# One decoder layer on one core: other row groups in the opening, part of its sums added by VectorE, and all its turns made by spaced transfers

## The chip, the cores and the metric

The kernel runs on one core of one Trainium2 chip. The metric is the device time in microseconds (us) of one launch. TensorE (PE) multiplies into PSUM; VectorE (DVE) and ScalarE (ACT) do elementwise work; GpSimd (POOL) does a few multiplies and issues some transfers; SyncE (SP) issues nearly all DMA transfers from one queue, in the order of the program.

## The reference

One layer for 256 tokens of width 2048 in float32. Every sub-layer is modulated by columns that are computed from a vector c through the large matrix w_ada (2048 x 9*2048).

```
mod = (silu(c) @ w_ada + b_ada).reshape(9, 2048)
h = rms_norm(x) * (1 + mod[1]) + mod[0]
x = x + 0.5 * mod[2] * swiglu(h, w_ffn1_gu, w_ffn1_down)     # d_ff = 5632
h = rms_norm(x) * (1 + mod[4]) + mod[3]
x = x + mod[5] * token_mixing(h, w_in, ...)                  # retention beside window attention
h = rms_norm(x) * (1 + mod[7]) + mod[6]
x = x + 0.5 * mod[8] * swiglu(h, w_ffn2_gu, w_ffn2_down)
out = rms_norm(x)

def swiglu(h, w_gu, w_down):
    gate, up = split(h @ w_gu, 2)
    return (silu(gate) * up) @ w_down
```

## The kernel before

Every large product is made in three parts. A weight tile (128 rows x 512 columns, two row blocks at a time) is split into a high half, cast by ScalarE (`wh`, L375), and a low half, subtracted by VectorE (`wl`, L377). The activations are held in the same two halves (`hh`, `hl`), and TensorE adds high by high, low by high and high by low into a bank of PSUM (`products`, L360). A row block is 128 of the 2048 rows of h; it takes six products of 512 columns per chunk of 512 output columns (three parts, two token tiles).

The columns of `mod` are made by VectorE: a row of w_ada (transposed, 1024 KB) is loaded and multiplied with silu(c) and summed (`ada_pass`, L220), in one, two or four passes of 2048, 1024 or 512 elements.

The first SwiGLU cannot start with the whole of h, since each row block of h needs its own two rows of `mod` (m = 1 and 0). So its first 16 chunks (eight pairs of gate and up, `EARLY = 8`) are opened in groups of row blocks. `bounds` says which blocks a group holds. In each group, every chunk is visited once (`visit`): the group's blocks are loaded (`load_blocks`, up to four blocks in a raw buffer), split and multiplied into the chunk's two banks. After a group but the last, the sums are copied out of PSUM by ScalarE (`to_parts`, L1219), and in the next group they are copied back into the banks ahead of the products (`open_banks`, L1191; the name for it there is seeded). The last group adds the saved parts when it applies SwiGLU (`swiglu_up`). The first group leaves its last two chunks (1 and 0) in their banks, and the third its last two as well.

While a group is visited, the generator `group` prepares the row blocks of the next one: it loads the rows of w_ada into the two halves of one slot (`ring`), makes the passes, and modulates the normed and transposed x. The transposed x comes from TensorE for the blocks below `TURNED` (`turned_x`) and from a load of transposed x with a multiply on GpSimd for the others (`normed_columns`).

The rows of the other columns (`ROWS_FFN1`: 3 x 16 rows of four passes, 192 passes) are spread over the work by `set_pace` and `tick`: each tick adds a rate, and each whole step is one pass. Before, the third group makes 48 of them, using one half of `ring`, and the last group 16 more, from raw buffers; the remaining 128 are spread over 117 halves of the chunks of `ffn_up` and the down product that follow.

`swiglu_up` has two ways to turn its result for the down product. With `by_dma`, ScalarE takes the two 16-bit planes of a tile apart (L535), SP issues a DMA transpose (L540), and ScalarE puts the planes together (L551); `later` spreads these steps over the following visits by `turn_step`. Otherwise TensorE transposes it (L518). Before, the first six of the eight pairs use DMA and the last two TensorE.

The order of SP is that of the program. The other engines' order outside a few parts written by hand is laid out by a planner from its own estimate of times; `tc.issue_after` only puts an instruction behind another. Pools: four raw buffers of 1 MB, three weight buffers, four banks of PSUM for sums, four slots, five `t512` tiles, three `flat` and four `back` tiles.

Of the kernel before, what the change touches and what calls it, by code (L numbers as in the profile page):

```python
# [9 lines left out]
F32 = mybir.dt.float32  # L10
# [3 lines left out]
ALU = mybir.AluOpType  # L14
# [3 lines left out]
P = 128  # L18
# [59 lines left out]
def layer_kernel(  # L78
# [55 lines left out]
    def t512():  # L134
        return tmp.tile([P, CH], F32, tag="t512", name=nm("t"))
# [497 lines left out]
    def parts_of_h(held, k, h):  # L633

        h = h.rearrange("p (k s) -> p k s", s=S)
        nc.scalar.copy(held.hi[:, k : k + 2, :], h)
        nc.vector.tensor_sub(held.lo[:, k : k + 2, :], h, held.hi[:, k : k + 2, :].bitcast(F32))

    def add_gated(bank, t, c0, gate, ssq):

# [10 lines left out]
    def later(work, then=None, quick=False):  # L651

        (a0, t0, m0), (a1, t1, m1) = work
        order = [a0, a1, None, None, None, t0, t1, None, m0]
        for f in order[:7] + order[7 + quick :]:
            yield
            if f is not None:
                f()
        m1()
        if then is not None:  # L660
            then()

    def later_by_pairs(work):

# [30 lines left out]
    def swiglu_up(banks_g, banks_u, tiles, ci, parts=None, by_dma=False, behind=None):  # L695

        k0 = ci * KB
        dest = tiles[k0 // KD].rearrange("p (k s) -> p k s", s=S)
        kk = k0 % KD
        work = []  # L700
        for t in range(NT):
            s = t512()
            g, u = banks_g[t], banks_u[t]
            if parts is not None:
                nc.vector.tensor_add(s, g, parts[0][t])
                nc.vector.tensor_add(parts[1][t], u, parts[1][t])
                g, u = s, parts[1][t]
            with nullcontext() if behind is None else tc.issue_after(behind):
                nc.scalar.activation(s, g, AF.Silu)
            nc.vector.tensor_mul(s, s, u)  # L710
            if by_dma:
                work.append(turn_by_dma(dest[:, kk : kk + KB, t * P : (t + 1) * P], s))
                continue
            transpose_to(
                dest[:, kk : kk + KB, t * P : (t + 1) * P],
                lambda j: s[:, j * P : (j + 1) * P],
                KB,
            )
        if work:
            turns.append(later(work))  # L720

    def ffn_up(held, w, tiles, first, bg=None, turned=(), ahead=None):
        for ci in range(first, DFF // CH):
# [252 lines left out]
        return [part[(n - 2) // 4][:, at + t * CH : at + (t + 1) * CH] for t in range(NT)]  # L976

    early = [ada_sums() for _ in range(2)]
    rows_of, alone = {}, [False]

    def place(m, k):
        if k < 1:
            rows_of[m, k] = raw_row()
        else:
            if not alone[0]:
                ring.reverse()
            rows_of[m, k] = ring[0]
        ada_load(m, k, rows_of[m, k], 2 if k < 2 else 1)

# [33 lines left out]
            op0=ALU.mult, op1=ALU.add, accum_out=dest,  # L1023
        )

    def turned_x(k0):

        xn = [t512()[:, : 2 * P] for _ in range(NT)]
        for t in range(NT):
            nc.scalar.mul(xn[t], x_sb[:, t, k0 * P : (k0 + 2) * P], r[:, t : t + 1])  # L1030
        turned = [bank()[:, :S] for _ in range(2)]
        for i in range(2):
            for t in range(NT):
                nc.tensor.transpose(
                    turned[i][:, t * P : (t + 1) * P], xn[t][:, i * P : (i + 1) * P], ident
                )
        return turned

    TURNED = 6
    root_row = []  # L1040

    def roots_in_rows():
# [9 lines left out]
            nc.tensor.matmul(rows_ps[:, :S], full, diag[:, :S], start=True, stop=True)  # L1052
        nc.scalar.copy(root_row[0], rows_ps[:, :S])

    def normed_columns(k0):

        xt = t512()
        both = xt.rearrange("p (k s) -> p k s", s=S)
        nc.sync.dma_start(both, x_t[k0 : k0 + 2].rearrange("k p s -> p k s"))
        nc.gpsimd.tensor_tensor(  # L1060
            out=both, in0=both, in1=root_row[0][:, None, :].broadcast_to([P, 2, S]), op=ALU.mult
        )
        return [xt[:, i * S : (i + 1) * S] for i in range(2)]

    def group(ks, passes=2):

        for k0 in ks[::2]:
            srcs = normed_columns(k0) if k0 >= TURNED else None
            for k in (k0, k0 + 1):
                for m in (1, 0):  # L1070
                    if (m, k) not in rows_of:
                        place(m, k)
                    for q in range(passes):
                        ada_pass(k, rows_of[m, k], early[m], q, passes)
                    yield
            for m in (1, 0):
                ada_end(m, slice(k0, k0 + 2), early[m], 0 if m else None, passes)
            h = t512()
            for i, src in enumerate(srcs or turned_x(k0)):
                modulated(h[:, i * S : (i + 1) * S], k0 + i, src, 0)  # L1080
            parts_of_h(held, k0, h)

    banks, moved, unlinted, fresh = {}, set(), set(), set()
    for n, one_bank in zip(firsts, (acc_bank, side_bank)):
        banks[n] = [one_bank() for _ in range(NT)]

# [17 lines left out]
    with tc.manual_schedule(engines=ORDERED):  # L1104
# [41 lines left out]
        modulated(h[:, S:], 1, first_x[1], 0)  # L1146
        parts_of_h(held, 0, h)
        whole_products(1, h)
    bounds = (0, 2, 6, 12, 16)
    groups = [range(a, b) for a, b in zip(bounds, bounds[1:])]  # L1150


# [27 lines left out]

    def open_banks(n, sums):
        seeded = sums and n in moved
        banks[n] = [acc_bank() for _ in range(NT)]
        unlinted.discard(n)
        fresh.add(n)
        if seeded:
            unlinted.add(n)
            fresh.discard(n)
            for b, p in zip(banks[n], part_of(n)):
                with tc.issue_after(cast[-1]):  # L1190
                    nc.scalar.copy(b, p)  # L1191
# [23 lines left out]

    def to_parts(n):
        for p, b in zip(part_of(n), banks.pop(n)):
            with tc.issue_after(cast[-1]):
                nc.scalar.copy(p, b)  # L1219
        moved.add(n)  # L1220

    ROWS_FFN1 = [(2, None, 0.5), (4, 1, None), (3, None, None)]
# [2 lines left out]
    def place_row():  # L1225
        return row_ring[0]() if row_ring else raw_row()

    def place_early():
        if row_ring:
            return row_ring[0]()  # L1230
        return ring[1] if alone[0] else raw_row()

    for g, ks in enumerate(groups):
        alone.append(g == len(groups) - 2)
        del alone[:-1]
        final = g == len(groups) - 1
        if g == len(groups) - 2:
            set_pace(ROWS_FFN1, 192, place_early, 0)
        if final:
            pace["rate"], pace["ahead"] = 1.0, 1  # L1240
        order = chunks if (len(groups) - g) % 2 else chunks[::-1]
        coming = iter(()) if final else group(groups[g + 1], 1 if g == 0 else 2)
        due = 0 if final else 2 * len(groups[g + 1])
        stay = () if final else order[-2:]
        for i, n in enumerate(order):
            if g == 0 and n in firsts:
                continue
            visit(n, ks, n not in stay, g == len(groups) - 2 or final and i < 8, final or (g == len(groups) - 2 and n in stay))
            if g:
                after = [(m, ks) for m in order[i + 1 : i + 2]]  # L1250
                if not after and not final:
                    after = [(n, groups[g + 1])]
                for m, ms in after:
                    ready(m, ms)
                    if m not in banks and not final:
                        open_banks(m, not (g == len(groups) - 2 and m in stay))
            if final:
                turn_step()
            last = len(order) - 2
            if g == 0:  # L1260
                by = [min(due, -(-j * due // 12)) for j in (i - 2, i - 1)]
                by = by[1] - by[0]
            else:
                by = (i + 1) * due // last - i * due // last if i < last else i == last
            for _ in range(by + (g == 0 and i == last)):
                next(coming, None)
            if g == 0:
                for m in {2: firsts[:1], 3: (order[2], firsts[1])}.get(i, order[i - 1 : i]):
                    if m not in stay:
                        to_parts(m)  # L1270
                if i == 3:
                    columns_rest()
                if i == 5:
                    roots_in_rows()
            if n in stay or g == 0:
                continue
            if not final:
                to_parts(n)
            elif n % 2:
                swiglu_up(  # L1280
                    banks.pop(n - 1),
                    banks.pop(n),
                    tiles,
                    n // 2,
                    (part_of(n - 1), part_of(n)),
                    n // 2 < 6,
                    cast[-1],
                )
    gate = gate_row()
    tiles.append(slot())  # L1290
    row_ring.append(two_rows())
    pace["rate"] = (192 - 64) / 117
    pace["ahead"] = AQ
    ffn_up(held, gu, tiles, EARLY, turned=range(EARLY, DFF // CH))
    gate_in = gate_load(gate, 2)
# [473 lines left out]
```

## Time and profile before

| | us |
|---|---|
| median of three timed executions | 2367.28 (2357.96, 2367.28, 2367.73) |
| the profiled execution | 2357.64 |
| its span, first to last instruction | 2355.5 |
| TensorE busy | 2335.7 (99%) |
| VectorE busy | 1673.1 (71%) |
| ScalarE busy | 1367.2 (58%) |
| read from HBM | 598.47 MB, 256 GB/s over the span |

Busy times are shares of the span, and the duration of a pipelined product overlaps the next one's. A window's row gives for each engine the busy us and, in brackets, the number of instructions, then TensorE's granted clock (1.00 is full speed), the mean busy share of the 16 DMA engines and the GB/s they moved. A group of instructions is told by line, engine, operation and tile, then busy us and mean ns of one, then the idle time just before them and what ended it. A wait's row has total us, times and the longest.

### The profile page before, as it was taken

To read this page: it belongs to the slowest core of one execution; us is meant where nothing else is said; L and a number is where in the kernel's file an instruction comes from. 1 tells how busy PE (TensorE), PEld (TensorE's weight loads), DVE (VectorE), ACT (ScalarE), POOL (GpSimd) and SP (SyncE) were. 2 spreads that over 40 slices of the span, in tenths; PEclk is the share of its full clock that TensorE was granted. 3 is DMA by queue.
4 is the path that set the end of the run, shared out by engine and by line. 5 is a ranking of instruction groups with operands and counts; after the bars stand their busy time and mean duration, and the time that the engine had idled before them with its cause. 6 is when DMAs were issued, how large, how long until landed. Compare 5 with 4: busy or idle time off the path is not lost.

```text
span 2355.5 us, 28357 instructions
## 1 busy us (share of the span) xinstructions
PE 2335.7 (99%) x10445; PEld 1918.6 (81%) x10445; DVE 1673.1 (71%) x2576; ACT 1367.2 (58%) x1888; POOL 18.3 (1%) x27
## 2 busy tenths in 40 slices
PE   8999999999999999999999999999999999999998
PEld 5888888888888888778888888888888888888887
DVE  7788888778867768976777776676555555555656
ACT  6766567455556567774556564465455454455544
POOL 0000000000000000000000000000000000000000
PEclk9999999999999999999999999999999999999999
DMA  9989889988765889876778787754767768666553
GB/s 383 375 323 361 355 294 328 336 306 293 302 237 220 293 267 255 258 212 254 267 273 306 288 310 281 272 204 179 259 237 256 242 239 268 223 231 202 193 197 125
DMA packets 191901, 630.24 MB, mean 268 GB/s; under 512 B 113105, under 2 KB 114769, under 8 KB 121233
## 3 DMA queue, kind: packets, MB, share of 16 engines
q1 hardware_dynamic: 189266, 617.41, 74.6%
q0 software_dynamic: 1600, 9.83, 1.0%
q8 instruction: 82, 1.34, 0.2%
q10 hardware_dynamic: 896, 1.19, 0.1%
q14 instruction: 57, 0.47, 0.1%
HBM read 598.47 MB, written 4.22 MB: 256 GB/s over the span
## 4 chain that ended last, share of the span: by engine, by line
PE 96%; DMA 2%; DVE 1%; ACT 1%; issue 0%; SPq 0%; DVEq 0%; ACTq 0%
PE pa L360 93%; DMA raw<-in_w_ffn_gu_dram 1%; DMA rows_x<-in_w_ada_dram 1%; PE ps L1453 0%; DVE slot L220 0%; PE pd L1369 0%; DVE wl L377 0%; ACT wh L375 0%; DMA x_sb<-in_x_dram 0%; PE ps L360 0%; PE pa L1099 0%; PE ps L895 0%; PE pd L1099 0%; DVE rows_x L220 0%; PE ps L1369 0%
## 5 line engine op out<-in xcount | busy, mean ns | idle before, releaser
L377 DVE TENSOR_TENSOR wl<-raw,wh 128x1024 fp32r<-128x1024 f32 x792 | 963.5, 1225 | 511.0 <-ACT wh L375 451.6
L375 ACT CAST wh<-raw 128x1024 fp32r<-128x1024 f32 x792 | 830.6, 1054 | 818.7 <-PE pa L360 752.6
L360 PE MATMUL pa<-wh,hh 128*128 128x512 f32 x2184 | 597.0, 391 | 3.0 <-ACT wh L375 1.7
L360 PE MATMUL pa<-wh,hl 128*128 128x512 f32 x2184 | 592.6, 389 | 0.0
L360 PE MATMUL pa<-wl,hh 128*128 128x512 f32 x2184 | 586.2, 390 | 0.2
L360 PEld LDWEIGHTS pa<-wh,hh 128*128 128x128 f32 x2184 | 407.5, 188 | 91.6 <-ACT wh L375 2.9
L360 PEld LDWEIGHTS pa<-wl,hh 128*128 128x128 f32 x2184 | 409.4, 188 | 86.7 <-DVE wl L377 1.0
L360 PEld LDWEIGHTS pa<-wh,hl 128*128 128x128 f32 x2184 | 409.8, 188 | 86.1 <-issue 0.4
L360 PE MATMUL pa<-wh,a 128*128 128x512 f32 x1824 | 452.1, 389 | 0.0
L360 PEld LDWEIGHTS pa<-wh,a 128*128 128x128 f32 x1824 | 341.7, 188 | 70.6
L360 PE MATMUL pa<-wl,a 128*128 128x512 f32 x912 | 245.1, 389 | 0.0
L220 DVE CUSTOM_DVE_ANT_0 slot<-slot,cact 128x512 f32<-128x512 f32 (+2 forms) x288 | 219.3, 812 | 30.0 <-DMA slot<-in_w_ada_dram 29.5
L360 PEld LDWEIGHTS pa<-wl,a 128*128 128x128 f32 x912 | 171.1, 188 | 35.4
L551 ACT COPY slot<-back 128x512 uint16<-128x512 uint16 x148 | 98.7, 766 | 0.0
L220 DVE CUSTOM_DVE_ANT_0 rows_x<-rows_x,cact 128x512 f32<-128x512 f32 x124 | 78.7, 686 | 18.0 <-DMA rows_x<-in_w_ada_dram 17.8
L410 ACT CAST a<-slot 128x512 fp32r<-128x512 f32 x114 | 70.6, 620 | 29.3 <-PE pa L360 29.0
L535 ACT COPY flat<-t 128x512 uint16<-128x512 uint16 x136 | 76.7, 617 | 8.9 <-DVE t L1526 5.7
L411 DVE TENSOR_TENSOR a<-slot,a 128x512 fp32r<-128x512 f32 x114 | 77.8, 684 | 0.3 <-ACT a L410 0.3
L220 DVE CUSTOM_DVE_ANT_0 raw<-raw,cact 128x512 f32<-128x512 f32 (+1 forms) x92 | 60.7, 709 | 14.6 <-DMA raw<-in_w_ada_dram 14.5
L1219 ACT COPY slot<-pa 128x512 f32<-128x512 f32 x72 | 38.6, 589 | 21.2 <-PE pa L360 21.0
L360 PE MATMUL pa<-wh,home 128*128 128x512 f32 x160 | 39.5, 389 | 0.0
L220 DVE DVE_READ_ACCUMULATOR2_ANT sums<- 128x1 f32 x440 | 35.9, 82 | 0.0
(232 smaller groups left out, 1087.0 us busy)
## 6 DMA issues: line engine op xcount, KB each, us to landing
raw<-in_w_ffn_gu_dram SPq DMA_DIRECT2D x160, 1024.0 KB, 5.5
raw<-in_w_in_dram SPq DMA_DIRECT2D x104, 1024.0 KB, 5.8
raw<-in_w_ffn_down_dram SPq DMA_DIRECT2D x88, 1024.0 KB, 4.9
slot<-in_w_ada_dram SPq DMA_DIRECT2D x87, 1024.0 KB, 7.4
rows_x<-in_w_ada_dram SPq DMA_DIRECT2D x31, 1024.0 KB, 7.1
raw<-in_w_ada_dram SPq DMA_DIRECT2D x22, 1024.0 KB, 5.7
raw<-in_w_swa_branch_dram SPq DMA_DIRECT2D x16, 1024.0 KB, 5.0
raw<-in_w_ret_branch_dram SPq DMA_DIRECT2D x16, 1024.0 KB, 5.4
```

Source lines behind the costliest of these rows:

```text
L220: nc.vector.tensor_tensor_reduce(out=w[:, at], in0=w[:, at], in1=cact[:, at], scale=1.0, scalar=0.0, op0=ALU.mult, op1=ALU.add, accum_out= ...
L360: product = nc.tensor.matmul(banks[t], act[:, j, t * P : (t + 1) * P], weights[:, j, :], start=starts and i == 0 and j == 0, stop=ends and ...
L375: cast.append(nc.scalar.copy(hi, src).ins)
L377: low.append(nc.vector.tensor_sub(lo, src, hi.bitcast(F32)).ins)
L410: nc.scalar.copy(hi, v)
L411: nc.vector.tensor_sub(lo, v, hi.bitcast(F32))
L535: nc.scalar.copy(planes[:, i, :], words(src)[:, :, i])
L551: nc.scalar.copy(into[:, :, :, i], held["turned"][:, i])
L1219: nc.scalar.copy(p, b)
```

## The change

- The groups of row blocks are (2, 3, 4, 7) instead of (2, 4, 6, 4). `parts_of_h`, `turned_x`, `normed_columns` and `group` take one block where a group has an odd number; `TURNED` is 5 instead of 6.
- In the second group, the chunks `chunks[1::3]` (1, 4, 7, 10, 13) are not copied back into PSUM if they were saved; their new sums are added to the saved ones by VectorE in `to_parts`.
- All eight pairs are turned by DMA transposes, and the opening's steps follow `evenly`, which spreads them over eight visits.
- The third group makes no passes of `ROWS_FFN1`, and the coming rows always alternate between both halves of `ring`. The last group makes 32 passes, at half a pass for each piece of a visit; the remaining 160 are spread over the same 117 halves.

```
+    def evenly(work):
+        (a0, t0, m0), (a1, t1, m1) = work
+        for fs in ((), (a0,), (t0, a1), (t1,), (), (), (m0,), (m1,)):
+            for f in fs:
+                f()
+            yield
...
         if work:
-            turns.append(later(work))
+            turns.append((later if behind is None else evenly)(work))
...
     def place(m, k):
...
-            if not alone[0]:
-                ring.reverse()
+            ring.reverse()
...
-    TURNED = 6
+    TURNED = 5
...
     def group(ks, passes=2):
         for k0 in ks[::2]:
-            srcs = normed_columns(k0) if k0 >= TURNED else None
-            for k in (k0, k0 + 1):
+            nk = min(2, ks[-1] + 1 - k0)
+            srcs = normed_columns(k0, nk) if k0 >= TURNED else None
+            for k in range(k0, k0 + nk):
...
-    bounds = (0, 2, 6, 12, 16)
+    bounds = (0, 2, 5, 9, 16)
...
         seeded = sums and n in moved
+        if seeded and n in by_vector:
+            added.add(n)
+            seeded = False
...
     def to_parts(n):
         for p, b in zip(part_of(n), banks.pop(n)):
+            if n in added:
+                with tc.issue_after(low[-1]):
+                    nc.vector.tensor_add(p, p, b)
+                continue
             with tc.issue_after(cast[-1]):
                 nc.scalar.copy(p, b)
+        added.discard(n)
         moved.add(n)
...
-        if g == len(groups) - 2:
-            set_pace(ROWS_FFN1, 192, place_early, 0)
+        by_vector = chunks[1::3] if g == 1 else ()
         if final:
-            pace["rate"], pace["ahead"] = 1.0, 1
+            set_pace(ROWS_FFN1, 2 * 192, place_row, 1)
...
-            visit(n, ks, n not in stay, g == len(groups) - 2 or final and i < 8, final or (g == len(groups) - 2 and n in stay))
+            visit(n, ks, n not in stay, final, final or (g == len(groups) - 2 and n in stay))
...
                     (part_of(n - 1), part_of(n)),
-                    n // 2 < 6,
+                    True,
                     cast[-1],
...
-    pace["rate"] = (192 - 64) / 117
+    pace["rate"] = (192 - 32) / 117
```

More of the change, by code (lines that the diff above doesn't have):

```diff
@@ L635, in parts_of_h @@
         h = h.rearrange("p (k s) -> p k s", s=S)
-        nc.scalar.copy(held.hi[:, k : k + 2, :], h)
-        nc.vector.tensor_sub(held.lo[:, k : k + 2, :], h, held.hi[:, k : k + 2, :].bitcast(F32))
+        ks = slice(k, k + h.shape[1])
+        nc.scalar.copy(held.hi[:, ks, :], h)
+        nc.vector.tensor_sub(held.lo[:, ks, :], h, held.hi[:, ks, :].bitcast(F32))
     def add_gated(bank, t, c0, gate, ssq):
@@ L978, in layer_kernel @@
     early = [ada_sums() for _ in range(2)]
-    rows_of, alone = {}, [False]
+    rows_of = {}
     def place(m, k):
@@ L1024, in square, with turned_x @@
         )
-    def turned_x(k0):
-        xn = [t512()[:, : 2 * P] for _ in range(NT)]
+    def turned_x(k0, nk=2):
+        xn = [t512()[:, : nk * P] for _ in range(NT)]
         for t in range(NT):
-            nc.scalar.mul(xn[t], x_sb[:, t, k0 * P : (k0 + 2) * P], r[:, t : t + 1])
-        turned = [bank()[:, :S] for _ in range(2)]
-        for i in range(2):
+            nc.scalar.mul(xn[t], x_sb[:, t, k0 * P : (k0 + nk) * P], r[:, t : t + 1])
+        turned = [bank()[:, :S] for _ in range(nk)]
+        for i in range(nk):
             for t in range(NT):
@@ L1053, in roots_in_rows, with normed_columns @@
         nc.scalar.copy(root_row[0], rows_ps[:, :S])
-    def normed_columns(k0):
-        xt = t512()
+    def normed_columns(k0, nk):
+        xt = t512()[:, : nk * S]
         both = xt.rearrange("p (k s) -> p k s", s=S)
-        nc.sync.dma_start(both, x_t[k0 : k0 + 2].rearrange("k p s -> p k s"))
+        nc.sync.dma_start(both, x_t[k0 : k0 + nk].rearrange("k p s -> p k s"))
         nc.gpsimd.tensor_tensor(
-            out=both, in0=both, in1=root_row[0][:, None, :].broadcast_to([P, 2, S]), op=ALU.mult
+            out=both, in0=both, in1=root_row[0][:, None, :].broadcast_to([P, nk, S]), op=ALU.mult
         )
-        return [xt[:, i * S : (i + 1) * S] for i in range(2)]
+        return [xt[:, i * S : (i + 1) * S] for i in range(nk)]
     def group(ks, passes=2):
         for k0 in ks[::2]:
-            srcs = normed_columns(k0) if k0 >= TURNED else None
-            for k in (k0, k0 + 1):
+            nk = min(2, ks[-1] + 1 - k0)
+            srcs = normed_columns(k0, nk) if k0 >= TURNED else None
+            for k in range(k0, k0 + nk):
                 for m in (1, 0):
@@ L1076, in group @@
             for m in (1, 0):
-                ada_end(m, slice(k0, k0 + 2), early[m], 0 if m else None, passes)
-            h = t512()
-            for i, src in enumerate(srcs or turned_x(k0)):
+                ada_end(m, slice(k0, k0 + nk), early[m], 0 if m else None, passes)
+            h = t512()[:, : nk * S]
+            for i, src in enumerate(srcs or turned_x(k0, nk)):
                 modulated(h[:, i * S : (i + 1) * S], k0 + i, src, 0)
             parts_of_h(held, k0, h)
-    banks, moved, unlinted, fresh = {}, set(), set(), set()
+    banks, moved, unlinted, fresh, added = {}, set(), set(), set(), set()
     for n, one_bank in zip(firsts, (acc_bank, side_bank)):
@@ L1226, in place_row @@
         return row_ring[0]() if row_ring else raw_row()
[L1228 to L1231, printed above, removed]
     for g, ks in enumerate(groups):
-        alone.append(g == len(groups) - 2)
-        del alone[:-1]
         final = g == len(groups) - 1
-        if g == len(groups) - 2:
-            set_pace(ROWS_FFN1, 192, place_early, 0)
+        by_vector = chunks[1::3] if g == 1 else ()
         if final:
-            pace["rate"], pace["ahead"] = 1.0, 1
+            set_pace(ROWS_FFN1, 2 * 192, place_row, 1)
         order = chunks if (len(groups) - g) % 2 else chunks[::-1]
```

## The prediction

> **What bounds the kernel now.** I read the page's head and chain of waits first, then the table of what TensorE waited for, then windows cut by stage.
>
> ```profile
> span 2355.5 us, 28357 instructions
> ...
> PE 2335.7 (99%) x10445; PEld 1918.6 (81%) x10445; DVE 1673.1 (71%) x2576; ACT 1367.2 (58%) x1888; POOL 18.3 (1%) x27
> ...
> PE 96%; DMA 2%; DVE 1%; ACT 1%; issue 0%; SPq 0%; DVEq 0%; ACTq 0%
> ...
> PE ps L1034 <- ACT t L1030: 4.2, 1, 4.2
> PE pa L177 <- DMA c_row<-in_c_dram: 2.5, 1, 2.5
> PE pa L1099 <- ACT t L628: 1.8, 1, 1.8
> PE pa L360 <- ACT wh L375: 1.7, 3, 1.0
> PE pa L360 <- ACT a L410: 0.8, 1, 0.8
> PE pa L360 <- ACT pa L1191: 0.5, 1, 0.5
> ```
>
> TensorE is busy for 99% of the span and carries 96% of the chain. Of its named waits, the first three (8.5 us) come before the first split product and lie outside the diff. Only 1.7 and 0.5 us lie in the opening's grouped visits. So the change can win only idle time of TensorE there, or TensorE work that disappears. It can lose wherever another resource runs out. The stages, in us, with busy time of each engine, DMA share and GB/s:
>
> ```profile
> 27.00:64.00 37.00, 35.21 (x155) 27.38 (x154) 31.67 (x36) 27.09 (x44) 0.00 (x0) 1.00 0.99 388
> 64.00:151.00 87.00, 87.00 (x384) 72.01 (x385) 72.43 (x100) 66.81 (x101) 4.58 (x3) 1.00 0.92 360
> 151.00:282.00 131.00, 130.49 (x575) 107.63 (x575) 107.22 (x187) 76.31 (x106) 4.25 (x2) 1.00 0.89 352
> 282.00:378.00 96.00, 96.00 (x429) 79.44 (x428) 84.90 (x133) 69.05 (x95) 2.16 (x4) 1.00 0.88 292
> 378.00:540.00 162.00, 162.00 (x720) 134.26 (x720) 123.19 (x216) 88.93 (x107) 0.00 (x0) 1.00 0.92 326
> 27.00:40.00 13.00, 13.00 (x59) 10.30 (x58) 11.48 (x15) 9.47 (x15) 0.00 (x0) 1.00 1.01 413
> 80.00:100.00 20.00, 20.00 (x90) 16.57 (x89) 16.91 (x25) 14.49 (x23) 1.38 (x1) 1.00 1.00 397
> ```
>
> The first four rows are roughly the groups of 2, 4, 6 and 4 row blocks. Group one has its DMA engines full (0.99) and TensorE idle for 1.8 us; in the others TensorE hardly pauses, though DMA share is about 0.9 and VectorE is up to 88% busy (84.90 of 96). A product takes 87.00/384 = 0.227 us. A visit of a chunk does 6 products per block: 2.7 us for 2 blocks, 4.1 for 3, 5.4 for 4, 9.5 for 7.
>
> How much is lost in the opening as a whole:
>
> ```profile
> 26.95 1.48 PE L360 MATMUL pa<-wh,hh 128*128 128x512 f32 x4
> ...
> 48.59 1.19 PE L360 MATMUL pa<-wh,hh 128*128 128x512 f32 x4 [0.30 <-ACT wh L375]
> ...
> 63.87 1.20 PE L360 MATMUL pa<-wl,hh 128*128 128x512 f32 x4
> ...
> 377.82 1.28 DVE L706 TENSOR_TENSOR a<-pa,a 128x512 f32<-128x512 f32 x2
> ...
> 372.10 0.44 PE ps L518 x4
> ...
> 373.45 0.44 PE ps L518 x4
> ...
> 385.02 0.87 PE ps L518 x8
> ```
>
> From the first split product (26.95) to the read of the last chunk (377.82) are 350.9 us. The work is 14 chunks x 12 products in group one and 16 x 6 for each of 14 more blocks: 168 + 1344 = 1512, at 0.227 us 343.2. Some 25 small transposes and alike at 0.11 (0.44/4) are 2.7. So about 5 us are lost in all, and most of that in group one: that is the most that waits can give back.
>
> **The change part by part.**
>
> *Less TensorE work.* The last two chunk pairs were turned by TensorE: 16 transposes, 0.44 + 0.44 + 0.87 = 1.75 us in the chain. They go to DMA transposes: -1.75. TURNED 6 to 5 removes the two transposes of block 5: -0.2, against one more small load of x and GpSimd multiply. The product count does not change.
>
> *Group one with 6 rows of w_ada beside it instead of 8.* The rows are 1024 KB (1.05 MB), a chunk's two blocks 0.52 MB: before 14 x 0.52 + 8 x 1.05 = 15.7 MB, after 13.6 MB, in 38.2 us (168 x 0.227): 411 GB/s wanted before, 356 after. The first window reached 388 at share 0.99, so the stage asked for more than it got, and now asks for less. VectorE has two whole-row passes (2 x 1.218 us, priced below) less. Bounds: nothing to the 3.4 us that I attribute to it (the four products at 63.87 close the twelfth visit, at 64.7: 144 x 0.227 = 32.7 and 1.6 of small products took 37.8). I take -2.4, nearer the full end, since both the DMA engines and VectorE are relieved; what is late next is the cast that shares ScalarE with the copies out of PSUM.
>
> *Group two with 3 blocks (65.4 us instead of 87).* Prices:
>
> ```profile
> L375 ACT CAST wh<-raw 128x1024 fp32r<-128x1024 f32 x34 | 35.7, 1060 | 8.7 <-PE pa L360 8.6
> L1219 ACT COPY slot<-pa 128x512 f32<-128x512 f32 x26 | 14.0, 591 | 11.5 <-PE pa L360 11.5
> L1191 ACT COPY pa<-slot 128x512 f32<-128x512 f32 x24 | 13.5, 601 | 0.0
> L636 ACT CAST hh<-t 128x512 fp32r<-128x512 f32 x3 | 1.9, 630 | 0.0
> L377 DVE TENSOR_TENSOR wl<-raw,wh 128x1024 fp32r<-128x1024 f32 x34 | 42.3, 1253 | 12.7 <-ACT wh L375 12.5
> L220 DVE CUSTOM_DVE_ANT_0 slot<-slot,cact 128x1024 f32<-128x1024 f32 x24 | 28.4, 1218 | 0.0
> L637 DVE TENSOR_TENSOR hl<-t,hh 128x512 fp32r<-128x512 f32 x3 | 2.1, 687 | 1.8 <-ACT hh L636 1.8
> L706 DVE TENSOR_TENSOR slot<-pa,slot 128x512 f32<-128x512 f32 x12 | 7.7, 683 | 1.5 <-PE pa L360 1.5
> ```
>
> A visit now splits a piece of two blocks and one of a single block: ScalarE 1.06 + 0.63 (taken from the 128x512 cast of L636), VectorE 1.25 + 0.69. ScalarE over the group: splits 27, 28 copies out and 28 in at 0.6 less what goes away, modulation 4. "Five chunks" are four in effect: chunk 1 is still in its banks from group one and has no saved part, so chunks 4, 7, 10 and 13 are added by VectorE. That takes 16 copies x 0.6 = 9.5 us from ScalarE and puts 8 adds x 0.683 = 5.5 us on VectorE. ScalarE: 54/65.4 = 83% (98% without the adds; 77% before, 66.8/87). VectorE: splits 31, 8 rows x 2.5 = 20, the rest 4, adds 5.5: 60, by the overlap that the row of before shows (72.4 busy where its groups add to 78) 56/65.4 = 86% (83% before). Both fit; the work hiding them is TensorE's own, but the three weight buffers now cover 2 to 4 us instead of 5.4, and an add queued behind a 2.4 us row pass frees the banks late for the next seed copy, for which a first product waits. Bounds: -0.5 (the wait on L1191 gone) to +5 (0.3 us in each of 16 visits, as the wait at 48.59). I take +0.8, near the low end, as TensorE lost nothing at 64 to 151 with the same chain of copies.
>
> *Group three with 4 blocks and 14 rows beside it.* Its 48 paced passes move away, and the coming rows get both halves of the ring. Loads: 16 x 1.05 + 14 x 1.05 + 7 x 0.13 = 32.4 MB in 87.2 us: 371 GB/s, against 360 at 64 to 151, which has the same visits with 12 rows. VectorE: 72.4 + 2 x 2.4 = 77/87 = 89%, as at 282 to 378. SP waits for a ring half until the passes before last are done; weight loads queue behind it, but one row a visit (5.4 us, two halves, so 10.9 us a turn) leaves room for landing (7.3 us) and 2.4 us of passes. Bounds: 0 to +2.8 (360 GB/s as a ceiling: 32.4/0.360 = 90.0). I take +0.3, nearer the short windows of 413 and 397 GB/s.
>
> By the Trainium skill, "DMA: Bandwidth & Descriptors", Specifications, HBM gives one core about 358 GB/s; an estimate by that page is 32.4/0.358 = 90.5 us, +3.3 in this stage. The trace disagrees for short stretches (413 over 13 us, 397 over 20 us) and has no stage of 80 us above 360, so that a long stage at 371 is untried here.
>
> *Last group of 7 blocks, transfers spaced.* 29.4 MB of weights and 8 rows (64 pieces at half a pass each are the 32 passes) in 152.6 us: 248 GB/s. VectorE: 16 x (3 x 1.22 + 0.69) + 48 x 0.683 for the pairs + 32 x 0.69: 124/152.6 = 81%. The spaced turn copies one row tile per visit instead of both in a burst, and a transpose on SP only follows a copy made a visit earlier. Rows share four buffers with two loads per visit, so a weight load can stand behind a row's passes; these are short (4 x 0.69). Cover is 9.5 us a visit. 0, bounds -0.5 to +1.
>
> *The rest of the rows.* 32 of 192 passes are done by then, not 64, so each half-chunk later carries 160/117 = 1.37 passes, not 1.09. DMA issues with KB and us to landing, the DMA transposes from 378 to 520, the passes from 500 to 600, and VectorE's waits from 378 to 700:
>
> ```profile
> slot<-in_w_ada_dram SPq DMA_DIRECT2D x13, 1024.0 KB, 7.3
> slot<-in_w_ada_dram SPq DMA_DIRECT2D x31, 1024.0 KB, 7.9
> L540 SPq DMA_TRANSPOSE back<-flat x7: 1231/1353/3692, 381.3 to 518.8; - x7
> L220 DVE CUSTOM_DVE_ANT_0 slot<-slot,cact 128x512 f32<-128x512 f32 x40 | 25.3, 687 | 8.7 <-DMA slot<-in_w_ada_dram 8.7
> ...
> DVE wl L377 <- ACT wh L375: 48.2, 47, 1.9
> DVE slot L220 <- DMA slot<-in_w_ada_dram: 16.6, 13, 3.1
> ```
>
> The first row is 64 to 151, the second 362 to 700; a pass takes 25.3/40 = 0.63 us back to back. In 378 to 540 (59 half-chunks) 0.274 x 59 = 16 passes are 4.2 MB more: 326 to 352 GB/s. At 415 GB/s that is 0.06 of share on 0.92, and two more DMA transposes at about 2 us (an estimate: 52.8 MB at 415 GB/s fills 0.79 of the window, and seven issues and their neighbours the rest) bring 0.02: 1.0, full. VectorE gets 16 x 0.63 us: 123 to 133, 82%. TensorE lost nothing here although VectorE waited 16.6 us for rows. Bounds: 0 to +6 (the shortage if the share wanted were 1.04); I take +0.5, since four weight buffers stand in front.
>
> Sum: -1.75 - 0.2 - 2.4 + 0.8 + 0.3 + 0 + 0.5 = **-2.75 us**. The profiled execution took 2357.64 us (span 2355.5 and 2.1 around it): 2354.9. The median shown, 2367.28, is 9.6 above it: two of the three timed executions were at 2367 and one at 2357.96, and no row tells what those 9.6 are. I forecast against the median: **2364.5**. Changes under 0.5% (11.8 us) cannot be told from none.
>
> **The rivals.**
> *Late loads make the 9.6 us too.* If the longer executions lose their time where DMA is full, above all at 27 to 64, thinning that group takes it: 2367.28 - 9.6 - 2.75 = 2354.9, faster by 0.52%. For it: share 0.99 there. Against: only 5 us of loss are seen in the opening.
> *Nothing moves.* Short pieces in group two eat what group one gives: +2.4 - 0.4 on the sum, about 2366.5.
> *Long stages are capped at 360 GB/s.* Group three runs 2.8 us longer: 2367.0. The skill's 358 named above is this rule; the trace bears it out only in that no long stage passes 360.
> *Slower: rows arrive late after the opening.* VectorE takes rows and splits in one order; a row period shrinks from 10.0 to 8.0 us, of which 18% (1.4 us) is free, and DMA is full. The mean wait for a row is now 16.6/31 = 0.54 us. Beyond 1.4 us TensorE pays the excess on 40 rows; slower by 0.5% begins at 11.8 + 2.75 = 14.6 us, a mean wait of 1.8. At 2.0 us it is 24 us, less the sum's gains: about 2388. Against: the median landing would have to rise by over 1.2 us, from 7.9.
>
> **How the numbers follow.** Forecast 0.48; 9.6 us gone too, 0.21; nothing moves, 0.15; cap, 0.08; late rows, 0.08. Faster 0.21, slower 0.08, same 0.71. Range: below, the rival of 2354.9 with all 5 us of loss removed instead of 2.4, and 1.95 of transposes, is 2350.7; above, the median with the upper bounds of group two and the later rows (+5, +6) less 4.3: 2374. I give 2350 to 2374.
>
> **What would show it.** Right: no L518 in the opening; TensorE idle under 1 us in group one with DMA share under 0.95; eight adds in to_parts writing the saved parts; the last chunk read about 3 us earlier than 377.82; VectorE near 82% and no TensorE idle at 378 to 540. Wrong: TensorE waiting for L375 or L1191 in group two; weight loads landing after 10 us in group three; VectorE's waits for rows well over 1.4 us each.

## The result, and the profile after

| | before | after |
|---|---|---|
| median, us | 2361.03 (6 runs) | 2385.09 (6 runs) |
| ratio | | 1.0099, interval 1.0079 to 1.0118 |
| profiled execution, us | 2357.64 | 2387.15 |
| span, us | 2355.5 | 2385.1 |

The change costs 24 us by these medians and 29.5 us between the two profiled executions. Runs of before shared later with the experiments lie at 2357, some 28 us away. The forecast was 2364.5 in a range of 2350 to 2374: wrong in size and in sign.

Where it went is found with a mark that both kernels pass: the stretch of 430 products without a pause early in the token mixing. First before, then after, from the chains (start, length, what):

```profile
768.37 97.49 PE pa L360 x430
```

```profile
799.01 97.49 PE pa L360 x430
```

All 30.6 us are lost ahead of it. The waits of TensorE in the kernel after, whole run (total us, times, longest), have grown in one row above all, from 1.7 to 21.6:

```profile
PE pa L360 <- ACT wh L375: 21.6, 12, 4.1
```

The windows by stage (group one; two; three; last group in three parts; the first loads of the next chunk, of four row blocks each, and what follows):

```profile
27.00:64.00 37.00, 36.24 (x160) 28.89 (x159) 29.35 (x34) 28.53 (x47) 0.00 (x0) 1.00 0.91 343
64.00:130.00 66.00, 65.53 (x290) 53.88 (x289) 54.91 (x84) 47.93 (x76) 3.10 (x2) 1.00 0.93 349
130.00:218.00 88.00, 88.00 (x390) 72.88 (x389) 79.17 (x117) 66.58 (x100) 6.71 (x4) 1.00 0.93 368
218.00:300.00 82.00, 82.00 (x364) 67.89 (x363) 60.57 (x97) 42.81 (x54) 0.00 (x0) 1.00 0.82 268
300.00:340.00 40.00, 38.69 (x170) 31.37 (x169) 27.47 (x43) 22.56 (x33) 0.00 (x0) 1.00 0.62 211
340.00:374.00 34.00, 30.84 (x134) 24.56 (x133) 22.50 (x32) 22.66 (x34) 0.00 (x0) 1.00 0.74 235
374.00:426.00 52.00, 35.65 (x127) 27.25 (x126) 25.66 (x50) 22.64 (x33) 0.00 (x0) 0.87 0.72 223
426.00:520.00 94.00, 94.00 (x410) 77.50 (x409) 74.22 (x138) 50.40 (x61) 2.17 (x4) 0.98 0.99 361
```

Groups one to three run about as forecast. The end of the last group, 300 to 374, loses 4.5 us, and the last chunk of the opening is read at 380.05, not about 3 us earlier than 377.82, as the forecast had it, but 2.2 us later. The hole is at 374 to 426: TensorE is busy for 35.65 of 52 us, at a clock of 0.87, and not because anything is full: DMA moves 223 GB/s, VectorE and ScalarE stand half idle. (Later, at 520 to 700, TensorE loses 2.1 us more.) The chain in the hole repeats every 10.1 us:

```profile
383.44 1.04 ACT wh L375
384.49 1.30 ACT slot L551 x2
385.79 1.01 ACT flat L535 x2
386.79 0.26 SPq L540
...
387.10 0.02 SPq L351
...
387.14 5.35 DMA raw<-in_w_ffn_gu_dram
...
393.55 1.04 ACT wh L375
...
396.90 0.26 SPq L540
...
397.25 5.12 DMA raw<-in_w_ffn_gu_dram
```

As the chain has it, a weight load lands, ScalarE casts it, puts the planes of an older tile together (L551), takes a younger tile apart (L535), SP issues a transpose (L540), and only then the next weight load. TensorE needs 5.4 us for one load and gets one every 10.1 us. SP's own queue shows the alternation (start, us, instruction):

```profile
375.85 0.53 SPq L351 DMA_DIRECT2D raw<-in_w_ffn_gu_dram  x1
376.43 0.43 SPq L215 DMA_DIRECT2D slot<-in_w_ada_dram  x1
385.81 1.24 SPq L540 DMA_TRANSPOSE back<-flat  x1
387.14 0.53 SPq L351 DMA_DIRECT2D raw<-in_w_ffn_gu_dram  x1
387.72 0.43 SPq L215 DMA_DIRECT2D slot<-in_w_ada_dram  x1
395.92 1.24 SPq L540 DMA_TRANSPOSE back<-flat  x1
397.25 0.53 SPq L351 DMA_DIRECT2D raw<-in_w_ffn_gu_dram  x1
```

Between 376.9 and 385.8 SP does nothing but wait for the transpose to be allowed. What does the transpose wait for? The profile's table of waits says, for 200 to 430:

```profile
SPq L540 <- ACT flat L535: 93.7, 10, 13.2
...
SPq L540 <- ACT slot L551: 10.6, 2, 7.7
```

That names the copy apart. ScalarE's own rows suggest another:

```profile
382.49 2.00 ACT L375 CAST wh<-raw 128x1024 fp32r<-128x1024 f32 x2 [5.44 <-DMA raw<-in_w_ffn_gu_dram]
384.39 1.40 ACT L551 COPY slot<-back 128x512 uint16<-128x512 uint16 x2
385.66 1.13 ACT L535 COPY flat<-t 128x512 uint16<-128x512 uint16 x2
```

The transpose starts at 385.81, right where L551 ends (384.39 + 1.40 = 385.79) and 0.15 us into L535, which here makes the data of the *next* transpose. The last transpose of the hole starts at 417.25, 0.03 us after an L551 ended (415.83 + 1.39 = 417.22), with no L535 beside it at all. L551 frees one of the four `back` tiles. In `evenly`, a pair's first transpose is in its third step and the step that frees its tile in its seventh; pairs follow each other two steps apart, so the pair after next wants that tile in that same step. All four tiles are always held, and a transpose waits for an L551 that stands behind the cast of the newest weights (`issue_after(cast[-1])`).

### The profile page after: what moved, and what is told of

It reads as the page before. It is cut to its first block, busy times and chain, and to the rows that moved or that the text cites. A ratio compares the mean times of both kernels' runs of the same rounds, so it can differ in the third digit from the quotient of the medians.

```text
span 2385.1 us, 28386 instructions
## 1 busy us (share of the span) xinstructions
PE 2343.4 (98%) x10427; PEld 1920.9 (81%) x10427; DVE 1679.2 (70%) x2610; ACT 1368.8 (57%) x1901; POOL 19.3 (1%) x28
## 4 chain that ended last, share of the span: by engine, by line
PE 92%; DMA 3%; ACT 2%; DVE 2%; issue 1%; SPq 0%; DVEq 0%; ACTq 0%
PE pa L360 90%; DMA raw<-in_w_ffn_gu_dram 2%; ACT slot L551 1%; ACT wh L375 1%; PE ps L1462 0%; DVE wl L377 0%; ACT flat L535 0%; DVE slot L220 0%; PE pd L1378 0%; DMA x_sb<-in_x_dram 0%; PE ps L360 0%; PE pa L1108 0%; PE ps L904 0%; PE pd L1108 0%; PE ps L1378 0%
## 5 line engine op out<-in xcount | busy, mean ns | idle before, releaser
L377 DVE TENSOR_TENSOR wl<-raw,wh 128x1024 fp32r<-128x1024 f32 (+1 forms) x808 | 963.0, 1202 | 542.3 <-ACT wh L375 474.0
L375 ACT CAST wh<-raw 128x1024 fp32r<-128x1024 f32 (+1 forms) x808 | 831.8, 1036 | 831.6 <-PE pa L360 763.8
L360 PE MATMUL pa<-wh,hh 128*128 128x512 f32 x2184 | 602.1, 393 | 22.6 <-ACT wh L375 21.6
L220 DVE CUSTOM_DVE_ANT_0 slot<-slot,cact 128x512 f32<-128x512 f32 (+2 forms) x274 | 209.4, 814 | 7.9 <-DMA slot<-in_w_ada_dram 7.8
L551 ACT COPY slot<-back 128x512 uint16<-128x512 uint16 x156 | 105.1, 766 | 0.0
L535 ACT COPY flat<-t 128x512 uint16<-128x512 uint16 x144 | 81.1, 615 | 8.3 <-DVE t L1535 5.5
L220 DVE CUSTOM_DVE_ANT_0 raw<-raw,cact 128x512 f32<-128x512 f32 (+1 forms) x108 | 70.7, 707 | 17.0 <-DMA raw<-in_w_ada_dram 17.0
```

Source lines behind the costliest of these rows:

```text
L220: nc.vector.tensor_tensor_reduce(out=w[:, at], in0=w[:, at], in1=cact[:, at], scale=1.0, scalar=0.0, op0=ALU.mult, op1=ALU.add, accum_out= ...
L360: product = nc.tensor.matmul(banks[t], act[:, j, t * P : (t + 1) * P], weights[:, j, :], start=starts and i == 0 and j == 0, stop=ends and ...
L375: cast.append(nc.scalar.copy(hi, src).ins)
L377: low.append(nc.vector.tensor_sub(lo, src, hi.bitcast(F32)).ins)
L535: nc.scalar.copy(planes[:, i, :], words(src)[:, :, i])
L551: nc.scalar.copy(into[:, :, :, i], held["turned"][:, i])
```

## The experiments

Three theories: (1) the return tiles, as above; (2) the copy apart, as the table of waits names it; (3) the rival that I had put on record for a slower outcome, rows that arrive late. Four edits of the kernel after.

**The old spacing.**

```
-            turns.append((later if behind is None else evenly)(work))
+            turns.append(later(work))
```

> The changed kernel with the old spacing (later) for the opening's turns; groups, VectorE's adds, all pairs by transfers and the passes stay. Theory 1 (return tiles): a transpose on SP waits for one of the four back tiles, which ScalarE frees (L551) only after it has cast the newest weights, and the next weight load stands behind the transpose; one load per turn of about 10 us. With later the tiles come free two steps ahead, so the 24 us go: 2358 to 2363. Theory 2 (the copy apart, L535, one step ahead of its transpose is what SP waits for): the same, 2358 to 2363. Theory 3 (late rows of w_ada at 1.37 passes a half): no change, 2382 to 2388.

Measured: 2358.94 us, ratio to before 1.0005 (0.9996 to 1.0014). The whole loss hangs on the spacing; (3) is out, since the later rows were the same. Theories 1 and 2 gave the same range, so this run does not part them.

**The freeing steps one visit earlier.**

```
-        for fs in ((), (a0,), (t0, a1), (t1,), (), (), (m0,), (m1,)):
+        for fs in ((), (a0,), (t0, a1), (t1,), (), (m0,), (m1,), ()):
```

> The changed kernel with the two steps that put the planes together (L551, which free the back tiles) one visit earlier; the copies apart and the transposes stay where they are. Theory 1: the tile that a transpose needs is freed a step before, the loop holds two loads instead of one (about 5 us a load against TensorE's 5.4), and nearly all goes: 2359 to 2366. Theory 2: the copy apart is as late as before, 2382 to 2388. Theory 3: 2382 to 2388.

Measured: 2358.04 us, ratio 0.9992 (0.9978 to 1.0006). This is the whole cure, 1 us under theory 1's range, with copies and transposes where they were. SP's queue in this run at the same place:

```profile
376.41 0.59 SPq L351 DMA_DIRECT2D raw<-in_w_ffn_gu_dram  x1
381.51 1.23 SPq L540 DMA_TRANSPOSE back<-flat  x1
382.83 0.56 SPq L351 DMA_DIRECT2D raw<-in_w_ffn_gu_dram  x1
383.49 0.39 SPq L215 DMA_DIRECT2D slot<-in_w_ada_dram  x1
388.89 1.24 SPq L540 DMA_TRANSPOSE back<-flat  x1
390.22 1.16 SPq L351 DMA_DIRECT2D raw<-in_w_ffn_gu_dram  x1
391.47 0.38 SPq L215 DMA_DIRECT2D slot<-in_w_ada_dram  x1
391.90 0.90 SPq L351 DMA_DIRECT2D raw<-in_w_ffn_gu_dram  x2
```

The loads are 6.4 and 7.4 us apart instead of 11.3 and 10.1, and two at once follow at 391.9. TensorE is busy for 49.55 of the 52 us at 374 to 426. The transposes now start where a copy apart ends (L535 ends at 381.49 and 388.87): with the tiles free in time, that copy is what they follow next, but here it costs little.

**The copies apart one visit earlier.**

```
-        for fs in ((), (a0,), (t0, a1), (t1,), (), (), (m0,), (m1,)):
+        for fs in ((a0,), (a1,), (t0,), (t1,), (), (), (m0,), (m1,)):
```

> The changed kernel with the copies apart (L535) one visit earlier, so that two steps lie between a copy and its transpose; transposes and the steps that free the back tiles stay. Theory 1: nothing changes, 2382 to 2388. Theory 2: the wait of SP goes, 2359 to 2366. Theory 3: 2382 to 2388.

Measured: 2384.12 us, ratio 1.0105 (1.0080 to 1.0131): nothing cured. Yet the table of waits of this run still names the copy apart as SP's longest wait:

```profile
SPq L540 <- ACT flat L535: 82.9, 9, 13.2
```

So theory (2) falls, and with it that row's reading: it names a ScalarE instruction that ended close to SP's, not the one that was needed. In this run too the transposes start where an L551 ends: at 404.39 and 415.62, after ends at 404.37 and 415.59, with no L535 beside them.

**The old number of passes in the last group.**

```
-            set_pace(ROWS_FFN1, 2 * 192, place_row, 1)
+            set_pace(ROWS_FFN1, 192, place_row, 1)
...
-    pace["rate"] = (192 - 32) / 117
+    pace["rate"] = (192 - 64) / 117
```

> The changed kernel with 64 passes in the last group and 128 spread later (1.09 a half), as before; everything else stays. Theory 3: the later rows are on time again, 2359 to 2366. Theories 1 and 2: no gain, 2382 to 2390, since SP waits for the same copies and has four more row loads in the last group.

Measured: 2390.21 us, ratio 1.0131 (1.0109 to 1.0153), just over the 2382 to 2390 that theories 1 and 2 gave. Fewer passes later help nothing; more in the last group cost some 5 us more.

**The spacing alone, on the kernel before** (`evenly` added there and used as in the change).

> The kernel before with one edit: the new spacing of the opening's turns (copy apart, transpose and putting together spread one row tile a visit). Theory 1: pairs 2 to 5 reuse the four back tiles, eight transposes stand before a load of 1 MB each in visits of 5.4 us, and a turn of the loop takes about 10 us: some 8 x 4.6 less what is prefetched, 25 to 37 us, so 2382 to 2394. Rival: the spacing alone is harmless and needed the longer groups or the denser rows to hurt, 2355 to 2362.

Measured: 2385.38 us, ratio 1.0113 (1.0087 to 1.0138), inside what theory 1 gave. In visits of 5.4 us with one load each, SP's queue now reads:

```profile
337.99 0.53 SPq L1166 DMA_DIRECT2D raw<-in_w_ffn_gu_dram  x1
348.30 1.24 SPq L540 DMA_TRANSPOSE back<-flat  x1
349.63 0.53 SPq L1166 DMA_DIRECT2D raw<-in_w_ffn_gu_dram  x1
357.29 1.24 SPq L540 DMA_TRANSPOSE back<-flat  x1
358.62 0.53 SPq L1166 DMA_DIRECT2D raw<-in_w_ffn_gu_dram  x1
```

One load in 9 to 12 us; TensorE is busy for 60.78 of the 75 us there:

```profile
325.00:400.00 75.00, 60.78 (x241) 46.21 (x239) 42.97 (x58) 42.24 (x63) 2.17 (x4) 0.93 0.59 169
```

Neither the longer groups nor the denser rows are needed for the loss.

**The last two pairs by TensorE again**, on the kernel after (`True` back to `n // 2 < 6`).

> The changed kernel with the last two pairs turned by TensorE again; the new spacing stays for pairs 0 to 5. Theory 1: the loop is then confined to visits of 9.5 us, which one turn of the loop nearly covers; the 21 us lost in the first half-chunks after the last group go, 1.75 us of transposes come back: 2360 to 2366. Rival (the loss is in the last group itself): 2378 to 2386.

Measured: 2365.14 us, ratio 1.0026 (1.0014 to 1.0038). Without transposes among the loads after the last group, 20 of the 28 us are gone. Of the other 8, TensorE's idle time in the visits of 9.5 us is 4.3 (1.4 at 300 to 340 and 2.9 at 340 to 374), and the transposes by TensorE are 1.75 (an estimate, from the chain of before); 2.1 more are idle at 374 to 426.

**What else the change is worth**, on the kernel with the freeing steps earlier. No chunk added by VectorE (`by_vector = ()`):

> The kernel with the freeing steps one visit earlier, with no chunk of the second group added by VectorE: chunks 4, 7, 10 and 13 are copied in and out by ScalarE as before. Theory S: ScalarE then has 64 us of work in a group of 65 us and TensorE waits for seeds and casts, 2360 to 2365. Rival: the copies fit and nothing changes, 2356 to 2359.

Measured: 2356.60 us, ratio 0.9994 (0.9983 to 1.0005). My theory S fell: ScalarE carries the copies, and what TensorE lost in group two goes. ScalarE is busy for 56.10 of 66 us there (85%; I had 98%), with the adds for 47.61 (72%; I had 83%). From 64 to 130 TensorE is busy 65.52 us with the adds (the first row) and all 66.00 without:

```profile
64.00:130.00 66.00, 65.52 (x289) 53.84 (x288) 54.51 (x83) 47.61 (x75) 4.38 (x3) 1.00 0.93 354
```

```profile
64.00:130.00 66.00, 66.00 (x293) 54.66 (x292) 51.51 (x76) 56.10 (x94) 5.32 (x3) 1.00 0.95 364
```

The old groups of 2, 4, 6 and 4 (with the rate set so that 32 passes still fall in the last):

> The kernel with the freeing steps one visit earlier, with groups of 2, 4, 6 and 4 as before (32 passes in the last group still). If the groups of 2, 3, 4 and 7 are what gives the opening its 1 to 2 us: 2358 to 2363. If the visits of 5.4 us in the last group make SP wait again for back tiles: above 2363. Rival (the groups are worth nothing): 2356 to 2358.

Measured: 2370.00 us, ratio 1.0051 (1.0035 to 1.0067). This kernel loses again: in SP's queue at 331 to 364 there is a transpose for every load of weights, and the loads come 6.1 us apart on average, where TensorE needs 5.4. It is not the tile this time, as I had expected: the transposes start where a copy apart ends (331.34 and 344.14, after L535 ended at 331.32 and 344.12). So this does not price the groups. That the short visits alone are to blame is argued, not shown: the 32 passes also fall into 87 us instead of 153, and denser rows in the last group cost time, as the next runs show.

Passes in the last group, 64 and 48 and 16 in place of 32:

> The kernel with the freeing steps one visit earlier (2358.04) and, besides, 64 passes in the last group and 128 later. Theory L: what is left of the loss is the later rows at 1.37 passes a half (TensorE idle 3.9 us from 380 to 742, DMA share 1.01 at 380 to 510); at 1.09 it goes, 2353 to 2356. Rival: the last group pays it back, as VectorE has 32 x 0.69 us more there, 124 + 22 of 153 us: 2358 to 2364.

> The same with 48 passes in the last group and 144 later (1.23 a half). Theory L: half of the loss goes, 2355 to 2357, without filling VectorE in the last group. Rival: no difference from 2358.

> The kernel with the freeing steps one visit earlier and 16 passes in the last group, 176 later (1.50 a half). If the 4.6 us that TensorE still loses from 375 to 742 come of the density of the later rows, they grow: 2360 to 2366. If rows in the last group are what costs (64 passes 2363.6, 48 2359.9, 32 2358.0), it goes on down: 2355.5 to 2357.5.

Measured: 2363.55 (1.0023; 1.0010 to 1.0035), 2359.87 (1.0006; 0.9995 to 1.0017) and 2356.22 us (0.9992; 0.9979 to 1.0005), against 2358.04 with 32. Theory L fell: denser later rows did not cost time, and 64 and 48 passes in the last group did. With these TensorE idles 3.6 and 3.9 us at 218 to 374. With 32 and 16 it does not idle there, and the 1.8 us between these two, no more than the spread of each kernel's runs, come after the last group (idle 4.6 and 2.6 us at 374 to 700). That the passes cost time by holding raw buffers that weight loads need in the last group is argued, not shown.

**All pairs by transfers on the kernel before, at the old spacing** (`n // 2 < 6` to `True`).

> The kernel before with all eight pairs turned by transfers at the old spacing, nothing else. If the 16 transposes are on the path as the chain has them: 1.75 us less, 2354.5 to 2356. If the two more pairs of transposes crowd the DMA engines where the first half-chunks load (share 0.94 at 380 to 510): 2357 to 2361.

Measured: 2355.77 us, ratio 0.9986 (0.9973 to 0.9998): the one part of the change whose interval leaves out 1, and the lowest median found, 0.14% below before (0.02 to 0.27%). The chain's 1.75 us, 0.07%, lie inside. The size is loose: the medians differ by 1.2 us, while the runs of before spread from 2355.95 to 2368.45.

## Why the prediction was wrong, point by point

- *Less TensorE work*, -1.75: right in kind. No L518 is left in the opening, and the last experiment has a gain of this order (1.2 us by medians).
- *Group one*, -2.4: right in kind, less in size. DMA share fell from 0.99 to 0.91 (343 GB/s; 356 was forecast) and TensorE's idle time from 1.8 to 0.8 us, under the 1 us named.
- *Group two*, +0.8: 0.5 us idle. The chunks are four (eight adds run at L1232), but the reason I gave for them, that ScalarE would be full without them, is refuted by the run without adds: the copies were priced too high.
- *Group three*, +0.3: nothing was lost, at 368 GB/s over 88 us. That ends the rival of a cap at 360. The figure of 358 GB/s in the Trainium skill ("DMA: Bandwidth & Descriptors", Specifications) does not bind this core here.
- *The last group, transfers spaced*, 0 with bounds of -0.5 and +1: this is the step that failed. It measured about +27 (kernel after against the freeing steps one visit earlier: 2385.09 and 2358.04). I checked that a transpose follows its copy by a visit, and did not ask who holds the tile that it writes. Four tiles, one taken per step and held for four, are a pool without a spare, freed by ScalarE behind the newest cast. I also took 9.5 us of visit as cover, while the last turn steps run on among loads that TensorE uses up in 5.4 us each. There 21 us went: four loads from 375.85 took 42.7 us (9.9 to 11.4 each) instead of 21.8, of which 16.4 us are TensorE's idle time and some 4.6 its slower clock. What is queued behind the waiting transpose stands in SP's queue: the next weight load, with no other load of these weights in flight.
- *The rest of the rows*, +0.5: DMA did fill (0.99 at 426 to 520, 1.0 forecast), and TensorE, which lost nothing there before, idles 2.1 us at 520 to 700, four times my figure and inside my bounds. But density is not shown as the reason: with the freeing steps earlier and 16 more passes moved later, it does not idle at 520 to 700.
- *The rival "slower: rows arrive late"* gave 2388, close to the time measured, by another mechanism. The old number of passes later cured nothing, so the nearness is chance. The chance of 0.08 for slower was too low because no rival had the transfers' order as its place.
- *The rival that the 9.6 us go too* rested on the two longer executions of before. More runs of before put its median at 2357 to 2361, so the forecast should have stood on the profiled execution. The gains that it added up, 2.75 us, do not show even with the spacing mended: 2358.04, against 2356.76 for before in the same round.

## What to carry to other kernels

When steps of several items are interleaved over one in-order queue, count for each pool how many buffers the schedule holds at once: with as many held as there are, each issue waits for the step that frees one, and everything behind it in the queue (here the weight loads) loses its lead. Then close the loop: add up load, cast, free, issue; if that is longer than the consumer's time per load, the consumer starves although no engine or transfer is full. A row of waits names a neighbour in time, so move that instruction alone before believing it.

## What the runs showed of the hardware that I had not expected

TensorE's granted clock can fall after a pause, and the length of the pause alone does not tell when. In the kernel after, four products of one kind take 1.07 us, but after waits of 3.35 and 4.10 us some take 1.9, while after 2.74 us they do not:

```profile
383.59 1.20 PE L360 MATMUL pa<-wh,hh 128*128 128x512 f32 x4 [3.35 <-ACT wh L375]
...
385.98 1.91 PE L360 MATMUL pa<-wl,hh 128*128 128x512 f32 x4
...
393.69 1.21 PE L360 MATMUL pa<-wh,hh 128*128 128x512 f32 x4 [2.74 <-ACT wh L375]
394.74 1.09 PE L360 MATMUL pa<-wh,hl 128*128 128x512 f32 x4
...
403.56 2.07 PE L360 MATMUL pa<-wh,hh 128*128 128x512 f32 x4 [4.10 <-ACT wh L375]
```

The windows show it as a clock of 0.72 at 384 to 390, 1.00 at 390 to 400 and 0.66 at 400 to 410:

```profile
384.00:390.00 6.00, 6.00 (x21) 4.74 (x20) 5.58 (x12) 3.30 (x6) 0.00 (x0) 0.72 0.51 109
390.00:400.00 10.00, 6.73 (x29) 4.87 (x27) 4.81 (x10) 4.29 (x6) 0.00 (x0) 1.00 0.71 237
400.00:410.00 10.00, 6.43 (x17) 5.10 (x18) 2.36 (x2) 4.29 (x6) 0.00 (x0) 0.66 0.59 104
```

At 374 to 426, 35.65 us of busy time at a clock of 0.87 lose some 4.6 us (0.13 of 35.65, an estimate), so such a pause is paid beyond its own duration. The Trainium skill, "TensorE: Matmul & The Clock Gate" ("Why this matters for your kernels"), says to leave no gap over about 3 us between bursts or the array falls to half its clock. The three waits above agree with it, but others here do not: after 2.92 us in the kernel after, products take up to 1.91 us again, and in the run with the spacing alone on the kernel before they do so after a wait of 2.11 us:

```profile
347.01 1.20 PE L360 MATMUL pa<-wh,hh 128*128 128x512 f32 x4 [2.11 <-ACT wh L375]
348.05 1.82 PE L360 MATMUL pa<-wh,hl 128*128 128x512 f32 x4
```

What decides between such a wait and the harmless one of 2.74 us, these runs do not show; a pause under 3 us is not safe by them.
